# A first modulation computed on TensorE, between the first products, instead of on VectorE

## The chip, the cores and the metric

The kernel runs on one core of one Trainium2 chip. The metric is the device time of one execution in microseconds (us), as the median of several runs. One core has a matrix engine (TensorE, PE in the profile; its weight loads are listed apart as PEld), a vector engine (DVE), an activation engine (ACT), a general engine (POOL) and a sync engine (SP), which here only issues loads from the chip's memory. Each engine works off its own instructions in a fixed order and waits on semaphores for the others.

## The reference

Two small transformers run one after the other on a sequence of 512 positions with 1024 features, two layers each, in float32. Only the first one matters here:

```python
def first_block(x, c, positions, ada_w, ada_b, norm1_g, w_in, b_in, ...):
    cond = jax.nn.silu(c)
    for l in range(DEPTH):                       # 2 layers
        mod = (cond @ ada_w[l] + ada_b[l])[:, None, :]
        sh1, sc1, g1, sh2, sc2, g2 = jnp.split(mod, 6, axis=-1)
        h = rmsnorm(x, norm1_g[l]) * (1 + sc1) + sh1
        x = x + g1 * hybrid_mixer(h, cos, sin, w_in[l], b_in[l], ...)
        h = rmsnorm(x, norm2_g[l]) * (1 + sc2) + sh2
        x = x + g2 * swiglu(h, w_ffn_in[l], w_ffn_out[l])
```

`hybrid_mixer` projects h with `w_in` and runs three kinds of attention. One of them picks its keys by scores of index queries `qi` (four blocks of 128 features) against one index key `ki`, both rotated by position (`partial_rope`). The modulation `mod` has 6 x 1024 values, 48 groups of 128; the first normalization needs 16 of the groups, `sh1` and `sc1`.

## The kernel before, in words

Activations lie transposed, features on the partitions in 8 tiles (k = 0 to 7) of 128, positions along the free axis. A product in float32 precision is done as three: every operand is split into a rounded part ("hi") and the rest ("lo"), and hi x hi, lo x hi and hi x lo are added up in PSUM (`mm3`, L497). A *unit* is one block of 128 output features: 8 tiles x 3 = 24 matmuls of 128x512. Weights come as `w_raw` in loads of 512 KB; ACT rounds them (`w_hi`), DVE takes the difference (`w_lo`).

The order of each engine's instructions is written by hand: a list of `Op`s is worked off by `run_plan`, which lets weight preparation run ahead, and work that has to follow an evacuation at a distance is put off with `later(us, ...)` on a clock that the planner keeps. Buffers come from two arenas in SBUF, `ar` (57 slots of 512 rounded values) and `af` (45 slots of 256 values); `Slots.get` (L125) picks the free slot that was dropped first. Loads are issued on SP's queue in planned order, some on ACT's and POOL's.

The places that the change touches:
- `ada_ops` (L808): one group of `mod` is one load of 128 rows of the transposed `ada_w` (512 KB) and one DVE reduction over 128x1024 against `silu(c)`, which lies on all partitions (`spread_cond`). This is `CUSTOM_DVE_ANT_0` in the rows.
- `entry` (L1526), the start of layer 0. The input is loaded, transposed on PE and its row norms are made. Then for each tile k: two groups of `mod`, two small operations that make scale and shift (`ab`), one DVE multiplication of the tile (`norm_tile`, L741), the rounding on ACT and the lo part on POOL. `products` (L1544) holds the first five units together: 120 matmuls, three units for k = 0 and 1, then the other two, then all five tile by tile. These five units are `ki` and the four `qi`. Their first weights are prepared by ACT, DVE and POOL.
- `evac_turned` (L947): a `qi` unit that is done is copied out of PSUM by ACT and then rotated by `turn` (L936): four DVE multiplications of 32x512 by `sin_t` and two POOL operations with `cos_t`; `rest`, 6.5 us later on the planner's clock, splits it into hi and lo. In layer 1 the same units follow the end of layer 0.
- `spill` (L1136): the input tiles go to memory as `x_dram`, on POOL's queue.

The `Timed` helper records every operation, so all rows carry its line, L336 (L342 in the changed kernel); the rows are told apart by their tiles.

Of the kernel before, what the change touches and what calls it, by code (L numbers as in the profile page):

```python
# [98 lines left out]
ZO = 1  # L99
VG = 0  # L100
# [12 lines left out]
ROOM = 0  # L113


class Slots:


    def __init__(self, base, n, align=False):
        self.base, self.align = base, align  # L120
        self.free = [True] * n
        self.since = [0] * n
        self.now = 0

    def get(self, n=1):  # L125
# [3 lines left out]
        while i < len(self.free):  # L129
# [6 lines left out]
            for a in range(i, e - n + 1):  # L136
                if a % step == 0:
                    r = (a if n >= 8 else a < LOW and not self.align, self.broken(a, n) if self.align else 0,
                         max(self.since[a:a + n]))
                    if best is None or r < best[0]:  # L140
                        best = (r, a)
# [17 lines left out]
class Slot:  # L159
# [5 lines left out]
    def drop(self):  # L165
        for j in range(self.i, self.i + self.n):
            assert not self.pool.free[j]
            self.pool.free[j] = True
            self.pool.since[j] = self.pool.now = self.pool.now + 1
# [191 lines left out]
def tile_forward(ctx, tc, t, out):  # L361
# [13 lines left out]
    R, F = Slots(ar, NR, True), Slots(af, NF)  # L375

    def new(cols):
# [27 lines left out]
           (("m", 16), ("a0", 117), ("a1", 117), ("b0", 69), ("b1", 69))}  # L405
# [429 lines left out]
    def start_loads():  # L835
# [13 lines left out]
        columns("a0", 117, at=st["xs"][0].ap)  # L849
# [5 lines left out]
        spread_cond("cond", t["c"], q, False)  # L855
        st["load"](0, 2)
        st["load"](1, 3)
        st["hold"] = True
        rotary()

# [86 lines left out]
    def evac_turned(bias, dst, eng=None):  # L947
        def done(_, p):
            T = new(512)
            act(T.ap, p, AF.Identity, bias=bias)  # L950

            turn(T.ap, eng)
# [7 lines left out]
            later(6.5 if eng else 8.5, rest, dst)  # L960
# [185 lines left out]
    def block1_layer(l, ada, close):  # L1146
# [13 lines left out]
        def ki_done(_, p):  # L1160
            T, U = new(512), new(512)
            act(T.ap, p, AF.Identity, bias=vc[:, 77:78])
            later(1.5, lambda: ki_rest(T, U), ki)

        def ki_rest(T, U):
# [16 lines left out]
            later(7.0, rest, ki)  # L1182
# [343 lines left out]
    def entry(units):  # L1526

        vc = vec["a0"]
        def stats():
            act(scr, one_c, AF.Silu)  # L1530
            rows_stats(st["rows"], 0, junk, between)

        def between():
            act(st["cond"].ap, st["cond"].ap, AF.Silu)
            rows_turn(st.pop("rows"), st["x"], range(8))
        plan = [Op(0.0, start_loads), Op(0.0, stats), norm_spread(XW), Op(0.0, rotary_sin)]
        for u in units[:EP]:
# [5 lines left out]
        plan.append(Op(0.0, begin))  # L1543
        def products():  # L1544
# [3 lines left out]
            for k in range(2):  # L1548
                for u in units[:3]:
                    u.mms(k, k + 1, 0)  # L1550
            for u in units[3:]:
                u.mms(0, 2, 0)
            for k in range(2, 6):
                for u in units:
                    u.mms(k, k + 1, 0)
            for u in units:
                u.mms(6, KT, 0)
# [3 lines left out]
        def tile_op(k):  # L1561
            def run():
                nc.vector.scalar_tensor_tensor(ab[:, 0, k:k + 1], mod[:, 0, 8 + k:9 + k], 1.0, vc[:, k:k + 1],
                                               op0=OP.add, op1=OP.mult)
                nc.vector.tensor_copy(ab[:, 1, k:k + 1], mod[:, 0, k:k + 1])
                lo = norm_tile(XW, k, st["tmp"][k % 2].ap, st["tmp"][2 + k % 2].ap if k < HL else None)
                lo()
                if k == KT - 1:
                    st.pop("rx")
                    for s in st.pop("tmp"):  # L1570
                        s.drop()
            return Op(0.0, run)
        for k in range(KT):
            plan += ada(2 * k + 2, 16)
            plan.append(tile_op(k))
# [828 lines left out]
```

## Time and profile before

| | |
|---|---|
| median of 3 runs | 3311.58 us (3309.7 to 3319.43) |
| profiled execution | 3316.53 us, of which 3314.8 us from the first to the last instruction |
| PE busy | 3191.6 us (96%) |
| DVE busy | 2086.4 us (63%) |
| ACT busy | 1246.1 us (38%) |
| POOL busy | 526.8 us (16%) |
| mean granted TensorE clock | 0.978 of 2.4 GHz |

The page gives every engine's busy time, the span in 40 slices, the loads, the chain of work that ended last and the costliest groups. Its chain of waits is mostly PE: 56% of the span. PE is idle for 123 us of the span (3314.8 less 3191.6). A granted clock of 0.50 is 1.2 GHz, 1.00 is 2.4 GHz, and a stretch with a value between has some time at each.

### The profile page before, as it was taken

How to read it: one execution, taken by the hardware profiler on the slowest of the kernel's cores; microseconds unless marked ns; L12 is line 12 of the kernel's file. 1: busy time of each engine (PE TensorE's matmuls, PEld its weight loads, DVE VectorE, ACT ScalarE, POOL GpSimd, SP SyncE). 2: the span in 40 equal slices, each digit the busy share in tenths (PEclk: the TensorE clock that was granted, in tenths of full speed). 3: DMA queues.
4: the chain of work that ended last, by engine and by line, in shares of the span. 5: the costliest groups of instructions: out<-in, count | busy, mean ns of one | idle time of the engine just before them, and what ended most of it. 6: DMA issues, size and time to landing. Idle time of an engine off the chain costs nothing.

```text
span 3314.8 us, 42542 instructions
## 1 busy us (share of the span) xinstructions
PE 3191.6 (96%) x16663; PEld 2688.9 (81%) x16663; DVE 2086.4 (63%) x3632; ACT 1246.1 (38%) x2147; POOL 526.8 (16%) x431
## 2 busy tenths in 40 slices
PE   6899999999989999999999998899999999989999
PEld 4788788888878787798888887788888887778888
DVE  8777665566578864458885665566666655664443
ACT  4544324222245452242224454342222244543333
POOL 3233001000022410010002562100000046300001
PEclk8999999999999999999999999999999999999999
DMA  6211352465431112335553112133333221223222
GB/s 241 68 67 51 122 208 97 171 220 213 138 114 63 56 52 83 127 113 185 195 203 129 52 34 72 52 108 117 122 122 121 94 100 42 77 71 102 96 96 77
DMA packets 109068, 370.19 MB, mean 112 GB/s; under 512 B 12352, under 2 KB 13124, under 8 KB 108484
## 3 DMA queue, kind: packets, MB, share of 16 engines
q1 hardware_dynamic: 99778, 339.65, 29.7%
q0 software_dynamic: 5328, 20.97, 1.7%
q10 hardware_dynamic: 3762, 6.86, 0.7%
q8 instruction: 131, 2.15, 0.3%
q14 instruction: 69, 0.57, 0.1%
HBM read 354.85 MB, written 12.58 MB: 111 GB/s over the span
## 4 chain that ended last, share of the span: by engine, by line
PE 56%; DVE 5%; ACT 2%; issue 1%; POOL 0%; DMA 0%; ACTq 0%; DVEq 0%; POOLq 0%
PE ps L336 56%; DVE ar L336 2%; DVE af L336 2%; ACT af L336 1%; ACT ar L336 1%; DVE junk L336 1%; DVE w_lo L336 0%; ACT w_hi L336 0%; POOL af L336 0%; DMA w_raw<-in_win_dram 0%; DVE small L336 0%; DVE osum L336 0%; DMA af<-in_lam_dram 0%; ACT L336 0%; ACT osum L336 0%
## 5 line engine op out<-in xcount | busy, mean ns | idle before, releaser
L336 PE MATMUL ps<-ar,w_hi 128*128 128x512 f32 (+2 forms) x8248 | 2385.1, 371 | 48.7 <-DVE ar L336 23.3
L336 PEld LDWEIGHTS ps<-ar,w_hi 128*128 128x128 f32 (+1 forms) x8248 | 1499.9, 190 | 326.5 <-DVE ar L336 27.0
L336 PE MATMUL ps<-ar,w_lo 128*128 128x512 f32 (+2 forms) x4124 | 1512.3, 368 | 2.7 <-DVE w_lo L336 2.7
L336 PEld LDWEIGHTS ps<-ar,w_lo 128*128 128x128 f32 (+1 forms) x4124 | 782.4, 190 | 122.2 <-DVE w_lo L336 3.1
L336 DVE TENSOR_TENSOR w_lo<-w_raw,w_hi 128x1024 fp32r<-128x1024 f32 (+3 forms) x414 | 477.2, 1156 | 223.4 <-ACT w_hi L336 221.9
L336 ACT ACTIVATE w_hi<-w_raw 128x1024 fp32r<-128x1024 f32 (+3 forms) x452 | 440.1, 977 | 441.9 <-PE ps L336 391.8
L336 PE MATMUL ps<-ar 128*128 128x256 f32 (+6 forms) x3096 | 504.2, 331 | 28.2 <-ACT ar L336 13.8
L336 PEld LDWEIGHTS ps<-ar 128*128 128x128 f32 (+1 forms) x3096 | 423.0, 194 | 102.8 <-issue 19.0
L336 POOL TENSOR_TENSOR af<-af 128x512 f32<-128x512 f32 (+5 forms) x151 | 178.6, 1185 | 1646.3 <-ACT af L336 1623.2
L336 DVE SCALAR_TENSOR_TENSOR af<-ps,mod,af 128x512 f32<-128x512 f32 (+1 forms) x257 | 165.2, 646 | 263.9 <-PE ps L336 263.9
L336 ACT ACTIVATE ar<-af 128x512 fp32r<-128x512 f32 (+2 forms) x216 | 128.3, 599 | 439.4 <-DVE af L336 432.5
L336 ACT ACTIVATE af<-ps 128x512 f32<-128x512 f32 (+2 forms) x290 | 142.1, 516 | 376.1 <-PE ps L336 372.1
L336 DVE TENSOR_TENSOR ar<-af,ar 128x512 fp32r<-128x512 f32 (+2 forms) x202 | 144.5, 718 | 120.2 <-ACT ar L336 120.2
L336 DVE TENSOR_TENSOR ar<-ps,ar 128x512 fp32r<-128x512 f32 (+3 forms) x212 | 131.8, 648 | 84.8 <-ACT ar L336 84.1
L336 POOL TENSOR_TENSOR af<-af,sin_t 32x512 f32<-32x512 f32 x104 | 151.2, 1453 | 144.4 <-ACT af L336 61.8
L336 ACT ACTIVATE ar<-ps 128x512 fp32r<-128x512 f32 (+3 forms) x212 | 113.2, 568 | 98.6 <-PE ps L336 96.4
L336 DVE TENSOR_TENSOR af<-af 128x512 f32<-128x512 f32 (+2 forms) x130 | 80.4, 619 | 109.1 <-ACT af L336 104.4
L336 DVE CUSTOM_DVE_ANT_0 af<-af,vec_a 128x1024 f32<-128x1024 f32 x96 | 123.0, 1290 | 34.2 <-DMA af<-in_ada_w_dram 33.9
L336 ACT ACTIVATE af<-af 128x256 f32<-128x256 f32 (+2 forms) x134 | 70.7, 538 | 179.5 <-DVE af L336 162.9
L336 DVE CUSTOM_DVE_ANT_0 junk<-af,vec_b 128x1024 bf16<-128x1024 f32 x96 | 122.7, 1278 | 12.2 <-DMA af<-in_w_ada_dram 12.2
L336 DVE CUSTOM_DVE_ANT_0 af<-af,vec_b 128x1024 f32<-128x1024 f32 x96 | 123.3, 1285 | 3.4
L336 PE MATMUL ps<-ident,af 128*128 128x128 f32 (+2 forms) x733 | 104.6, 280 | 19.9 <-DMA af<-in_vec_a_dram 5.9
(128 smaller groups left out, 1702.5 us busy)
## 6 DMA issues: line engine op xcount, KB each, us to landing
w_raw<-in_win_dram SPq DMA_DIRECT2D x138, 512.0 KB, 3.3
af<-in_ada_w_dram SPq DMA_DIRECT2D x96, 512.0 KB, 4.4
af<-in_w_ada_dram SPq DMA_DIRECT2D x96, 512.0 KB, 4.4
w_raw<-in_wm_dram SPq DMA_DIRECT2D x96, 512.0 KB, 3.3
w_raw<-in_wfi_dram SPq DMA_DIRECT2D x88, 512.0 KB, 3.6
w_raw<-in_wfo_dram SPq DMA_DIRECT2D x48, 384.0 KB, 3.1
w_raw<-in_wm_dram SPq DMA_DIRECT2D x32, 320.0 KB, 3.3
x_dram<-af POOLq DMA_DIRECT2D x16, 512.0 KB, 4.2
```

The lines of the kernel that those rows point to most:

```text
L336: r = f(*a, **k)
```

## The change

The 16 groups of `sh1` and `sc1` of layer 0 are computed by matmuls. A new layout `ada_first` of the same weights has the contracted index on the partitions, so a group is eight matmuls with a 128x128 block of the weights as the stationary operand and one column of `silu(c)` (`cc`, part of the tile `small`) as the moving one: 128 matmuls of 128x1. All 16 results stand in one PSUM bank. They are written between the first products, two after each 128x512 matmul, and the products are placed tile by tile between the tile operations. The lo part of the tiles and of the first weights is made by DVE alone; POOL has none of it. `silu(c)` on all partitions, which the other groups still need, is loaded after the entry.

Besides, `evac_turned` puts off the `turn` of the four `qi` units by 0, 3, 6 and 9 us of the planner's clock, and `Slots` picks a slot by the time at which the planner expects it to be free. The second gives many tiles other slots all through the kernel.

```diff
-                    r = (a if n >= 8 else a < LOW and not self.align, self.broken(a, n) if self.align else 0,
+                    late = max(0.0, max(self.since[a:a + n]) - self.clocks.at["act"])
+                    r = (a if n >= 8 else a < LOW and not self.align, round(late, 1) if late > LATE else 0.0,
+                         self.broken(a, n) if self.align or n < 3 else a % 3 if n == 3 else 0, late,
                          max(self.since[a:a + n]))
                     if best is None or r < best[0]:
...
     def drop(self):
+        at = self.pool.clocks.ready((), (self.ap,))
         for j in range(self.i, self.i + self.n):
             assert not self.pool.free[j]
             self.pool.free[j] = True
-            self.pool.since[j] = self.pool.now = self.pool.now + 1
...
-        spread_cond("cond", t["c"], q, False)
-        st["load"](0, 2)
+        st["first"] = deque()
+        first_ada(2)
         st["load"](1, 3)
         st["hold"] = True
         rotary()
+    FIRST = [c for k in range(KT) for c in (8 + k, k)]
+    def first_ada(n):
+        while st.get("fetched", 0) < n:
+            i = st["fetched"] = st.get("fetched", 0) + 1
+            s = new(1024)
+            nc.sync.dma_start(s.ap, t["ada_first"][FIRST[i - 1]])
+            st["first"].append(s)
     def rows_stats(rows, sc, junk, between=None):
...
-    def evac_turned(bias, dst, eng=None):
+    def evac_turned(bias, dst, eng=None, wait=0.0):
         def done(_, p):
             T = new(512)
             act(T.ap, p, AF.Identity, bias=bias)
-
-            turn(T.ap, eng)
             dst.pair = Pair(R)
             h, l = dst.pair.hi, dst.pair.lo
...
-            later(6.5 if eng else 8.5, rest, dst)
+            def middle():
+                turn(T.ap, eng)
+                later(RE if eng else 8.5, rest, dst)
+            later(wait, middle, dst) if wait else middle()
         return done
...
-                        evac(vc[:, 64 + i:65 + i], box, *((nc.vector,) if 9 <= i < 13 else ())))
+                        evac(vc[:, 64 + i:65 + i], box, *((nc.vector, RW + RS * (i - 9)) if 9 <= i < 13 else ())))
...
     def entry(units):
         vc = vec["a0"]
+        cc = small[:, 224:232]
+        b1 = small[:, 232:240]
         def stats():
             act(scr, one_c, AF.Silu)
-            rows_stats(st["rows"], 0, junk, between)
-
-        def between():
-            act(st["cond"].ap, st["cond"].ap, AF.Silu)
-            rows_turn(st.pop("rows"), st["x"], range(8))
-        plan = [Op(0.0, start_loads), Op(0.0, stats), norm_spread(XW), Op(0.0, rotary_sin)]
-        for u in units[:EP]:
-            u.w.rest = (nc.vector, nc.gpsimd)
+            act(cc, vc[:, 117:125], AF.Silu)
+            nc.vector.tensor_scalar(b1, vc[:, 24:32], 1.0, None, op0=OP.add)
+            rows = st.pop("rows")
+            rows_stats(rows, 0, junk)
+            rows_turn(rows, st["x"], range(8))
         def begin():
-            st["tmp"] = [new(S) for _ in range(4)]
+            st["tmp"] = [new(S) for _ in range(2)]
+            first_ada(6)
             new_h()
...
             st["entry"] = False
+            st["mods"] = bank("st")
+            open_banks.add(turns["last"])
+            st["mods_at"] = turns["last"]
             for u, tg in zip(units, ["acc", "acc", "pv", "st", "st"]):
                 u.open(0, tg)
...
+        def modulate(k):
+            p = st["mods"]
+            for i in (2 * k, 2 * k + 1):
+                w = st["first"].popleft()
+                for j in range(KT):
+                    nc.tensor.matmul(p[:, i:i + 1], w.ap[:, 128 * j:128 * j + 128], cc[:, j:j + 1],
+                                     start=j == 0, stop=j == KT - 1)
+                    yield
+                w.drop()
+            first_ada(min(16, 2 * k + 8))
+        def products(k, us, other=()):
+            other = iter(other)
+            h, l = hm(k)
+            for u in us:
+                for j, (w, x) in enumerate(((u.w.h, h), (u.w.l, h), (u.w.h, l))):
+                    nc.tensor.matmul(u.ps[0], w[k], x, start=k + j == 0, stop=k == KT - 1 and j == 2)
+                    next(other, None)
+                    next(other, None)
+            for _ in other:
+                pass
+        def tile_op(k):
+            nc.vector.scalar_tensor_tensor(ab[:, 0, k:k + 1], st["mods"][:, 2 * k:2 * k + 1], b1[:, k:k + 1], vc[:, k:k + 1],
+                                           op0=OP.add, op1=OP.mult)
+            nc.vector.tensor_add(ab[:, 1, k:k + 1], st["mods"][:, 2 * k + 1:2 * k + 2], vc[:, 16 + k:17 + k])
+            norm_tile(XW, k, st["tmp"][k % 2].ap)()
+            if k == KT - 1:
+                st.pop("rx")
+                for s in st.pop("tmp"):
+                    s.drop()
+        hm = hmove(lambda: h_box["h"])
+        def last():
+            open_banks.discard(st.pop("mods_at"))
+            st.pop("mods")
             for u in units:
-                u.mms(6, KT, 0)
+                for k in (KT - 2, KT - 1):
+                    products(k, [u])
+                open_banks.discard(u.at[0])
                 u.w.drop()
                 u.done(0, u.ps[0])
...
+        def step(f, *a):
+            return Op(0.0, lambda: f(*a))
+        some, rest = units[:3], units[3:]
+        plan = [Op(0.0, start_loads), Op(0.0, stats), Op(0.0, begin), step(lambda: deque(modulate(0)))]
+        plan += [norm_spread(XW), step(tile_op, 0), Op(0.0, lambda: None, pre=[u.w for u in some])]
+        plan += [Op(0.0, lambda: st["load"](1, 5)), step(lambda: deque(modulate(1))), step(tile_op, 1)]
+        for k in range(KT - 2):
+            if k == 1:
+                plan += [Op(0.0, lambda: None, pre=[u.w for u in rest])]
+            if k == 2:
+                plan += [step(products, 0, rest), step(products, 1, rest)]
+            if k == 3:
+                plan += [Op(0.0, lambda: st.pop("hold")), Op(0.0, rotary_sin)]
+            plan.append(step(lambda k=k: products(k, some if k < 2 else units, modulate(k + 2))))
+            plan.append(step(tile_op, k + 2))
         plan += [Op(0.0, spill), Op(0.0, rotary_end)]
-        plan += [Op(26.0, products, [u.w for u in units]), Op(0.0, more_consts)]
+        plan += [Op(26.0, last, [u.w for u in units]), Op(0.0, more_consts), Op(0.0, lambda: spread_cond("cond", t["c"]))]
         return plan
...
-        order = [c for k in range(KT) for c in (8 + k, k)] + list(range(16, 48)) if l == 0 else range(48)
+        order = range(16 if l == 0 else 0, 48)
...
-    todo, done = deque(adas), [0]
+    todo, done = deque(adas), [16]
...
+    o["ada_first"] = lay(a["ada_w"][:1, :, :2048], 8)[0]
...
+        if l == 0:
+            o["vec_a0"] = np.concatenate([o["vec_a0"], v(a["c"])])
```

PE's first rows, before: the transposed column vectors and input tiles, the spread of the norms, and the 120 products in one piece, then the first of the next unit (`w_hi`).

```order
L336 MATMUL ps<-ident,af 128x117
L336 MATMUL ps<-ident,af 128x128 x32
L336 MATMUL ps<-ident,stat 128x128 x4
L336 MATMUL ps<-ar 128x512 x120
L336 MATMUL ps<-ar,w_hi 128x512
```

And now, where `small` is the tile that holds `silu(c)` and `af` the modulation's weights:

```order
L342 MATMUL ps<-ident,af 128x125
L342 MATMUL ps<-ident,af 128x128 x32
L342 MATMUL ps<-small,af 128x1 x16
L342 MATMUL ps<-ident,stat 128x128 x4
L342 MATMUL ps<-small,af 128x1 x16
L342 MATMUL ps<-ar 128x512
L342 MATMUL ps<-small,af 128x1 x2
```

Groups of 16 narrow matmuls (one tile's scale and shift) stand ahead of the norms, behind them, and then in pairs between the products of k = 0 to 5: nine products with 16 narrow ones for k = 0 and again for k = 1, then 12 products of the other two units in a row, then 15 with 16 for each of k = 2 to 5, and 30 products alone for k = 6 and 7.

DVE's rows after the entry in layer 0, before: weights' lo parts, all four turns but one in a row (`sin_t`, four operations each), two small constants, the index weights `wf`, the last turn, and the lo part of a value unit that frees its PSUM bank (`ar<-ps`).

```order
L336 TENSOR_TENSOR w_lo<-w_raw,w_hi 128x1024 x2
L336 TENSOR_TENSOR af<-af,sin_t 32x512 x16
L336 CAST cmask_b<-af 128x128
L336 CAST ident_b<-ident 128x128
L336 TENSOR_TENSOR w_lo<-w_raw,w_hi 128x1024
L336 COPY wf<-ps 128x64
L336 TENSOR_SCALAR wsc<-wf 128x32
L336 TENSOR_TENSOR af<-af,sin_t 32x512 x4
L336 SCALAR_TENSOR_TENSOR ar<-ps,vec_a_95,ar 128x512
```

And now:

```order
L342 TENSOR_TENSOR w_lo<-w_raw,w_hi 128x1024 x2
L342 TENSOR_TENSOR af<-af,sin_t 32x512 x4
L342 CAST cmask_b<-af 128x128
L342 CAST ident_b<-ident 128x128
L342 TENSOR_TENSOR w_lo<-w_raw,w_hi 128x1024
L342 COPY wf<-ps 128x64
L342 TENSOR_SCALAR wsc<-wf 128x32
L342 TENSOR_TENSOR af<-af,sin_t 32x512 x8
L342 SCALAR_TENSOR_TENSOR ar<-ps,vec_a_95,ar 128x512
L342 TENSOR_TENSOR w_lo<-w_raw,w_hi 128x1024
L342 TENSOR_TENSOR ar<-af,ar 128x512
L342 TENSOR_TENSOR af<-af,sin_t 32x512 x4
```

Twelve `sin_t` operations stand ahead of the first `ar<-ps` where 20 stood.

DVE at the start of layer 1, before, from the first turns to the lo part that frees a bank:

```order
L336 TENSOR_TENSOR af<-af,sin_t 32x512 x8
L336 TENSOR_TENSOR w_lo<-w_raw,w_hi 128x1024
L336 TENSOR_TENSOR af<-af,sin_t 32x512 x4
L336 COPY wf<-ps 128x64
L336 TENSOR_SCALAR wsc<-wf 128x32
L336 TENSOR_TENSOR af<-af,sin_t 32x512 x4
L336 TENSOR_TENSOR w_lo<-w_raw,w_hi 128x1024
L336 TENSOR_TENSOR af<-af,sin_t 32x512 x4
L336 TENSOR_TENSOR ar<-af,ar 128x512 x2
L336 TENSOR_TENSOR w_lo<-w_raw,w_hi 128x1024
L336 TENSOR_TENSOR ar<-af,ar 128x512
L336 COPY af<-af 64x512
```

And now, the same stretch:

```order
L342 TENSOR_TENSOR af<-af,sin_t 32x512 x4
L342 TENSOR_TENSOR w_lo<-w_raw,w_hi 128x1024
L342 COPY wf<-ps 128x64
L342 TENSOR_SCALAR wsc<-wf 128x32
L342 TENSOR_TENSOR af<-af,sin_t 32x512 x8
L342 TENSOR_TENSOR w_lo<-w_raw,w_hi 128x1024
L342 TENSOR_TENSOR ar<-af,ar 128x512
L342 TENSOR_TENSOR w_lo<-w_raw,w_hi 128x1024
L342 TENSOR_TENSOR af<-af,sin_t 32x512 x4
L342 COPY af<-af 64x512
L342 TENSOR_TENSOR ar<-af,ar 128x512 x2
L342 SCALAR_TENSOR_TENSOR ar<-ps,vec_a_95,ar 128x512
```

The second `w_lo` stands behind 12 turn operations instead of 16, and the `ar<-ps` behind 16 instead of 20.

## Rows read from the trace of the kernel before

**Rows 1.** Page, the span in 40 slices: PE busy, and granted clock.
```profile
PE   6899999999989999999999998899999999989999
PEclk8999999999999999999999999999999999999999
```

**Rows 2.** Windows: busy us of PE, PEld, DVE, ACT, POOL; clock, DMA share, GB/s.
```profile
0.00:20.00 20.00, 7.67 (x37) 6.79 (x37) 10.26 (x27) 13.72 (x21) 0.20 (x4) 0.89 0.87 325
20.00:40.00 20.00, 9.89 (x18) 5.10 (x18) 18.03 (x25) 7.12 (x12) 10.48 (x6) 0.50 0.59 215
...
sum 120.00, PE 83.35 PEld 63.61 DVE 95.69 ACT 54.57 POOL 41.09; mean PE 13.89 PEld 10.60 DVE 15.95 ACT 9.10 POOL 6.85
```

**Rows 3.** Timeline of DVE in the entry: start, us, count, [idle before <- releaser].
```profile
22.28 4.73 DVE L336 TENSOR_TENSOR ar<-w_raw,ar 128x512 fp32r<-128x512 f32 x3 [1.92 <-ACT ar L336]
...
41.94 3.15 DVE L336 TENSOR_TENSOR ar<-w_raw,ar 128x512 fp32r<-128x512 f32 x4 [1.92 <-ACT ar L336]
...
48.27 1.28 DVE L336 CUSTOM_DVE_ANT_0 af<-af,vec_a 128x1024 f32<-128x1024 f32 x1
...
50.68 1.25 DVE L336 SCALAR_TENSOR_TENSOR ab<-mod,vec_a 128x1 f32<-128x1 f32 x1
...
51.96 0.75 DVE L336 SCALAR_TENSOR_TENSOR af<-af,ab,ps 128x512 f32<-128x512 f32 x1
...
55.03 1.24 DVE L336 SCALAR_TENSOR_TENSOR ab<-mod,vec_a 128x1 f32<-128x1 f32 x1
```

**Rows 4.** Timeline of PE in the entry and right after it.
```profile
22.30 0.79 PE L336 MATMUL ps<-ar 128*128 128x512 f32 x1 [4.09 <-ACT ar L336]
...
43.34 18.49 PE L336 MATMUL ps<-ar 128*128 128x512 f32 x74 [0.58 <-DVE ar L336]
...
64.34 5.94 PE L336 MATMUL ps<-ar 128*128 128x512 f32 x25 [1.23 <-POOL ar L336]
70.12 0.39 PE L336 MATMUL ps<-ar,w_hi 128*128 128x512 f32 x1
```

**Rows 5.** Timeline of PE at eight narrow matmuls.
```profile
550.66 0.95 PE L336 MATMUL ps<-mean_c,af 128*128 128x1 f32 x8
551.48 0.36 PE L336 MATMUL ps<-ar,w_hi 128*128 128x256 f32 x1
```

**Rows 6.** Windows at two packs of 16 narrow matmuls, columns as in Rows 2.
```profile
1814.70:1818.00 3.30, 2.71 (x25) 2.66 (x24) 2.12 (x2) 2.25 (x5) 1.04 (x1) 0.98 0.05 20
1818.00:1821.40 3.40, 3.40 (x17) 3.40 (x17) 1.53 (x12) 0.30 (x1) 0.00 (x0) 0.50 0.83 281
```

**Rows 7.** Timeline after the entry: turns on DVE, and PE's wait.
```profile
66.96 17.17 DVE L336 TENSOR_TENSOR af<-af,sin_t 32x512 f32<-32x512 f32 x16 [0.46 <-ACT af L336]
...
91.53 0.79 PE L336 MATMUL ps<-ar,w_hi 128*128 128x512 f32 x1 [9.76 <-DVE ar L336]
...
92.12 0.63 PE L336 MATMUL ps<-ar,w_lo 128*128 128x512 f32 x1
...
92.55 1.05 PE L336 MATMUL ps<-ar,w_hi 128*128 128x512 f32 x2
```

**Rows 8.** Window of PE's first matmuls behind that wait.
```profile
91.50:98.00 6.50, 6.47 (x16) 5.12 (x17) 6.27 (x7) 0.74 (x2) 2.75 (x2) 0.54 0.26 83
```

**Rows 9.** Timeline of DVE at the start of layer 1.
```profile
964.75 4.74 DVE L336 TENSOR_TENSOR af<-af,sin_t 32x512 f32<-32x512 f32 x4
...
976.52 0.75 DVE L336 SCALAR_TENSOR_TENSOR ar<-ps,vec_a,ar 128x512 fp32r<-128x512 f32 x1
```

**Rows 10.** Timeline of PE at the start of layer 1.
```profile
964.77 0.80 PE L336 MATMUL ps<-ar,w_lo 128*128 128x512 f32 x1 [2.70 <-DVE w_lo L336]
...
977.32 0.80 PE L336 MATMUL ps<-ar,w_hi 128*128 128x512 f32 x1 [5.55 <-DVE ar L336]
```

**Rows 11.** Windows at the start of layer 1.
```profile
962.00:968.00 6.00, 3.30 (x9) 2.56 (x9) 5.90 (x6) 0.61 (x2) 3.86 (x2) 0.72 0.28 98
976.00:985.00 9.00, 7.68 (x25) 6.21 (x26) 4.89 (x6) 3.45 (x5) 0.00 (x0) 0.69 0.40 147
```

More of the change, by code (lines that the diff above doesn't have):

```diff
@@ L99 @@
 ZO = 1
+LATE = 1.0
+RW, RS, RE = 0.0, 3.0, 6.5
+KW, KE = 1.5, 7.0
 VG = 0
@@ L112, with __init__ @@
 L0, L1 = 5.0, 8.0
-ROOM = 0
+ROOM, FROOM = 0, 0
 class Slots:
-    def __init__(self, base, n, align=False):
+    def __init__(self, base, n, clocks, align=False):
         self.base, self.align = base, align
@@ L122, in __init__ @@
         self.since = [0] * n
-        self.now = 0
+        self.clocks = clocks
     def get(self, n=1):
@@ L168, in drop @@
             self.pool.free[j] = True
-            self.pool.since[j] = self.pool.now = self.pool.now + 1
+            self.pool.since[j] = at
 class Pair:
@@ L374, in tile_forward @@
     af = arena.tile([128, NF, 256], FT, name="af")
-    R, F = Slots(ar, NR, True), Slots(af, NF)
+    R, F = Slots(ar, NR, clocks, True), Slots(af, NF, clocks)
     def new(cols):
@@ L404, in tile_forward @@
     vec = {n: const.tile([128, k], FT, name="vec_" + n) for n, k in
-           (("m", 16), ("a0", 117), ("a1", 117), ("b0", 69), ("b1", 69))}
+           (("m", 16), ("a0", 125), ("a1", 117), ("b0", 69), ("b1", 69))}
     mod = const.tile([128, 2, 48], FT, name="mod")
@@ L848, in start_loads @@
                                        ap=[[0, 128], [1, S]]))
-        columns("a0", 117, at=st["xs"][0].ap)
+        columns("a0", 125, at=st["xs"][0].ap)
         nc.vector.memset(quarter, math.pi / 2.0)
@@ L1162, in ki_done @@
             act(T.ap, p, AF.Identity, bias=vc[:, 77:78])
-            later(1.5, lambda: ki_rest(T, U), ki)
+            later(KW, lambda: ki_rest(T, U), ki)
         def ki_rest(T, U):
@@ L1181, in rest @@
                 U.drop()
-            later(7.0, rest, ki)
+            later(KE, rest, ki)
         u_ki = Unit(W(win[13], keep=True, rest=None), hm, XS, ki_done)
@@ L1540, in begin @@
         def begin():
-            st["tmp"] = [new(S) for _ in range(4)]
+            st["tmp"] = [new(S) for _ in range(2)]
+            first_ada(6)
             new_h()
-        plan.append(Op(0.0, begin))
-        def products():
             st["entry"] = False
+            st["mods"] = bank("st")
+            open_banks.add(turns["last"])
+            st["mods_at"] = turns["last"]
             for u, tg in zip(units, ["acc", "acc", "pv", "st", "st"]):
                 u.open(0, tg)
[L1548 to L1555, printed above, removed]
+        def modulate(k):
[8 more added lines that the diff above has]
+            first_ada(min(16, 2 * k + 8))
@@ L1556, in products @@
+        hm = hmove(lambda: h_box["h"])
+        def last():
+            open_banks.discard(st.pop("mods_at"))
+            st.pop("mods")
             for u in units:
-                u.mms(6, KT, 0)
+                for k in (KT - 2, KT - 1):
+                    products(k, [u])
+                open_banks.discard(u.at[0])
                 u.w.drop()
                 u.done(0, u.ps[0])
[L1561 to L1572, printed above, removed]
@@ L1573, in entry @@
-        for k in range(KT):
-            plan += ada(2 * k + 2, 16)
-            plan.append(tile_op(k))
-            if k == 0:
-                plan.append(Op(0.0, lambda: None, pre=[u.w for u in units[:3]]))
-            if k == HW:
-                plan.append(Op(0.0, lambda: st["load"](1, 5)))
-            if k == HU:
-                plan += [Op(0.0, lambda: None, pre=[u.w for u in units[3:]]), Op(0.0, lambda: st.pop("hold"))]
+        def step(f, *a):
+            return Op(0.0, lambda: f(*a))
@@ L2257, in mixed @@
                         late = wait(o)
-                        if late < 0.15 or wait(f) > late or sum(R.free) < ROOM or sum(F.free) < ROOM:
+                        if late < 0.15 or wait(f) > late or sum(R.free) < ROOM or sum(F.free) < FROOM:
                             break
```

## The prediction

> **What bounds the kernel now.** I began with the page's slices: PE is busy nearly throughout, and only the first two slices stay well below [rows 1]. The windows then say how much is in the start: PE works 83.35 of the first 120 us, so 36.65 of its 123 idle us lie in under 4% of the span, and the clock is 0.50 all through 20 to 40 us [rows 2]. In a stretch like that the question is what PE waits for, so next came DVE's timeline there. One tile of the entry costs DVE two reductions of 1.28 us, a scale of 1.25, a copy and a multiplication of 0.75, and scale follows scale after 55.03 - 50.68 = 4.35 us [rows 3]. PE gets its products only as tiles come: the first at 22.30, a run without a break from 43.34, the next units' weights at 70.12 [rows 4]. Behind the entry DVE makes 16 turn operations in one go and PE waits 9.76 us [rows 7]; the same pattern returns in layer 1 with waits of 2.70 and 5.55 us [rows 10]. These places are what the change touches; over the rest of the span PE hardly stops.
>
> **Prices.** Eight matmuls of 128x1, each with its own 128x128 weights, took 551.48 - 550.66 = 0.82 us, 0.103 each, at full clock [rows 5]. In a window at 0.50 seventeen matmuls, half of them of that kind, filled 3.40 us: 0.20 each [rows 6]. A 128x512 matmul starts 0.43 after the one before at half clock (92.12 to 92.55) [rows 7], and 25 of them took 5.94 us at full clock, 0.238 with the last one's tail [rows 4]; half of 0.43 is 0.215, and I take 0.227 between.
>
> **The entry.** Removed are 16 reductions of 1.28 us, 20 us of DVE, and POOL's share of the lo parts. Added are 128 narrow matmuls: 13 us of PE at full clock, 26 at half. Three of DVE's operations per tile remain and the lo part joins them, at most 1.25 + 0.14 + 0.75 + 0.75 = 2.9 us where the period was 4.35 [rows 3], so DVE no longer sets the pace once the weights are split. PE does, and its clock decides:
> - The first 16 narrow matmuls stand ahead of the spread of the norms, at half clock 3.2 us; the first tile no longer waits for two reductions (2.56 us). I put the first product at 22.7, 0.4 later than before.
> - The second product stands behind a pair of narrow matmuls that write the bank DVE reads for the second tile's scale, and in DVE's queue that scale stands behind six lo parts of weights. Shared with POOL such a part took 4.73 / 3 = 1.58, alone 3.15 / 4 = 0.79 [rows 3]; POOL has none now, so six are 4.7 us and PE goes on at about 27.8. Nothing covers this wait.
> - k = 0 and k = 1: 9 x 0.43 + 16 x 0.20 = 7.1 us each at half clock, to 42.0.
> - Then 12 wide matmuls alone. Before, the clock came up in the unbroken run from 43.34: 74 products in 18.49 us, 0.25 each [rows 4]. I expect the same here: 12 x 0.43 = 5.2, with the rise near their end, to 46.8.
> - k = 2 to 5 at full clock: 15 x 0.227 + 16 x 0.103 = 5.05 each, to 67.0; the last 30 take 6.8, to 73.8.
> Before, this point came at 70.12: the entry gets 3.7 us longer. DVE's 20 us were not all on the path, PE had 36 us to spare, but the spare time lay where the clock was at 0.50.
>
> Loads: the third tile's two groups are the thirteenth load of 512 KB on SP; at 325 GB/s [rows 2] 6.8 MB take 21 us. The spill of the input tiles to memory (four writes of 512 KB) no longer stands behind POOL's lo parts and goes out among them; with it the sum is 8.9 MB and 27.4 us, just in time for 27.8. I take nothing for it; if the next four loads shared the time as well, 11.0 MB and 33.8 us, it would be 6 us late, the upper bound.
>
> **Behind the entry, layer 0.** PE's third unit needs the lo part that frees its bank, and 12 turn operations stand ahead of it on DVE instead of 20. One costs 17.17 / 16 = 1.07 us beside POOL [rows 7]: 8 x 1.07 = 8.6 us earlier, against a wait of 9.76. What is late next is the fourth unit: its lo parts now stand behind a bundle of four (4.3 us). I count half of that as given back, 8.6 - 2.1 = 6.5 gained. The bounds are 4.3 (all given back) and 11.8: 16 matmuls behind the wait ran at 0.54 [rows 8], and if the wait gets short enough for the clock to stay up, 16 x 0.20 = 3.2 come on top. The late load of silu(c) and its two ACT operations stand behind the entry while DVE sets the pace there, so nothing for them.
>
> **Layer 1.** The second lo part stands behind 12 turn operations instead of 16. At 4.74 / 4 = 1.19 us [rows 9] that is 4.7 us earlier, and the wait of 2.70 goes [rows 10]. The unit before then ends some 5 us sooner; on DVE come one lo part, one `w_lo`, the last bundle (4.7) and four short ones ahead of the `ar<-ps` that ended at 977.27 [rows 9]. Walking this queue I get 969.5 for it and 967.5 for PE: a wait of 2 us is left of 5.55, so 3.5 gained. In the windows there, 9 matmuls took 3.30 us and 25 took 7.68 [rows 11]; at 0.227 they would take 2.0 and 5.7, another 3.3 for the clock. Sum 9.5 us. Bounds: 2.7 (only the first wait) and 13.
>
> **The slots.** Other slots change waits all over the kernel. Outside the places above PE idles about 123.2 - 36.65 - 8.25 = 78 us, spread over many small waits that no rule here takes away or adds. I count 0, and 5% of it, 4 us, either way as an estimate.
>
> **Sum.** 3.7 - 6.5 - 9.5 + 0 = -12.3 us. On the profiled execution: 3316.53 - 12.3 = 3304.2. That execution was 4.95 us above the median of 3311.58, so the same saving from the median gives 3299.3; I predict 3299. What counts as no change is 0.3%, 9.9 us, so the forecast lies just past the edge.
>
> **Rivals.**
> - *The clock stays down in the entry; slower.* Place: the products of k = 2 to 5. If the 12 wide matmuls don't bring it to 1.00, or the narrow ones between push it back, each of four tiles costs 15 x 0.43 + 16 x 0.20 = 9.65 instead of 5.05, and about ten of the last 30 run at 0.43: 18.4 + 2.0 = 20.4 more, 3299.3 + 20.4 = 3319.7. It gets slower than before from the point where three of the four tiles run at half. For it: with a pack of narrow matmuls, PE busy 2.71 of 3.30 us, the clock went from 0.98 to 0.50 and stayed there while more of them were mixed in [rows 6]. Against it: in those packs nothing wide stood between, here one wide matmul takes as long as the two narrow ones, and the run ahead of them is wide alone. Chance 0.13.
> - *The clock rises at once; faster.* If it comes up within k = 0, some 3 us into it, the rest of k = 0 takes 2.3, k = 1 takes 9 x 0.227 + 16 x 0.103 = 3.7, the 12 take 2.7, and all from there as above: the end comes near 67, about 7 earlier, 3292. For it: PE has no idle time from 27.8 on. Against it: rows 6 again, and the half clock through 20 to 40 us in spite of short bursts [rows 2]. The Trainium skill speaks for this one: "TensorE: Matmul & The Clock Gate", Part 1 (the HAM clock gate), says that the gate is set by how busy PE has been recently, and a stream of narrow matmuls is busy. By that rule the time would be 3292; the trace does not agree, since PE was busy 82% of the window in which its clock was lost. Chance 0.15.
> - *The queue only moves.* DVE still has 20 turn operations to make before the index scores, and made 16 in 17.17 us without a break [rows 7]. If every bundle that leaves one place delays a `w_lo` or an `ar<-ps` at the next, only the first wait of layer 1 goes: 3311.6 + 3.7 - 2.7 = 3312.6. For it: in both layers the bundles still stand ahead of the lo parts in the order. Against it: from layer 1's third unit on PE has wide units of 24 matmuls, 5.4 us each, and a bundle is 4.3 to 4.7. Chance 0.18.
> - *The slots decide.* A wait of some 10 us appears or goes where no row points: 3289 or 3309. Chance 0.10, half each.
>
> **How the numbers follow.** The forecast's own case has 0.44, with its own range of 3291 to 3307: the bounds of the two turn terms, not all at once, and 4 us for the slots. In it the time is below 3301.7 (0.3% under the median) two times in three. Faster: 0.29 + 0.14 from the early clock + 0.06 from slots + 0.01 = 0.50. Slower: 0.07 from the late clock, 0.02 from the queue, 0.02 from slots = 0.11. The rest, 0.39, is within 0.3%. The range that leaves out about one in ten on each side goes from 3285, the early clock with the full gain behind the entry, to 3318, just short of the late clock.
>
> **What would show it.** In the profile after: the first product near 22.7 and the second near 27.8; the clock 0.50 until about 46 and 1.00 from there; the first `w_hi` product of the later units near 74; PE's wait behind the first two units at 2 to 4 us instead of 9.76; the first wait of layer 1 gone, the second about 2. The prediction is wrong if the granted clock is 1.00 before 40 or still 0.50 at 52, if a load releases the narrow matmuls, or if the waits on `ar<-ps` are as long as before.

## The result, and the profile after

The changed kernel takes 3347.1 us (median of 4 runs, 3345.59 to 3350.22) where the kernel before, timed beside it, takes 3315.51: a ratio of 1.0097 with a 95% interval of 1.0076 to 1.0119. 32 us slower, where 3299 was predicted and 3318 was the upper end of the range.

The page's slices look better than before, and that is the trap in them: PE is busy for 8 tenths of each of the first two slices, where [rows 1] had 6 and 8, but the granted clock is a tenth lower in both.

```profile
PE   8899999999999999999999998899999999989999
PEclk7899999999999999999999999999999999989999
```

The windows (columns as in [rows 2]) show PE without a pause from 20 to 100 us, and 106.71 us busy of the first 120 where 83.35 were needed before. The time is not lost in waits; PE has more to do, and much of it at half clock.

```profile
20.00:40.00 20.00, 20.00 (x88) 19.08 (x87) 7.15 (x14) 4.56 (x8) 0.00 (x0) 0.50 0.82 328
40.00:60.00 20.00, 20.00 (x85) 17.82 (x84) 5.92 (x12) 3.52 (x6) 0.00 (x0) 0.60 0.23 80
60.00:80.00 20.00, 20.00 (x122) 17.85 (x122) 5.26 (x12) 5.22 (x7) 0.00 (x0) 0.91 0.37 132
80.00:100.00 20.00, 20.00 (x90) 16.69 (x90) 7.97 (x14) 6.06 (x8) 2.57 (x2) 0.83 0.25 78
sum 120.00, PE 106.71 PEld 94.33 DVE 50.20 ACT 36.06 POOL 13.68; mean PE 17.79 PEld 15.72 DVE 8.37 ACT 6.01 POOL 2.28
```

PE's timeline in the entry, beside [rows 4], tells what it has to do. The reader should compare the counts with the order of the change: there a tile's pack is x16 and a pair is x2, here they are x32 and x4.

```profile
15.82 6.96 PE L342 MATMUL ps<-small,af 128*128 128x1 f32 x32 [2.86 <-ACT af L342]
22.64 1.09 PE L342 MATMUL ps<-ident,stat 128*128 128x128 f32 x4
23.53 6.83 PE L342 MATMUL ps<-small,af 128*128 128x1 f32 x32
30.22 0.77 PE L342 MATMUL ps<-ar 128*128 128x512 f32 x1
30.79 0.95 PE L342 MATMUL ps<-small,af 128*128 128x1 f32 x4
31.60 0.77 PE L342 MATMUL ps<-ar 128*128 128x512 f32 x1
...
51.23 5.64 PE L342 MATMUL ps<-ar 128*128 128x512 f32 x14
56.71 0.50 PE L342 MATMUL ps<-small,af 128*128 128x1 f32 x4
...
85.72 10.72 PE L342 MATMUL ps<-ar 128*128 128x512 f32 x37
96.28 0.39 PE L342 MATMUL ps<-ar,w_hi 128*128 128x512 f32 x1
```

The list of groups (busy us, mean ns) counts them all: 128 matmuls of the program stand in the trace as 256, each with a weight load of its own (PEld).

```profile
L342 PE MATMUL ps<-small,af 128*128 128x1 f32 x256 | 44.5, 285 | 2.9 <-ACT af L342 2.9
L342 PEld LDWEIGHTS ps<-small,af 128*128 128x128 f32 x256 | 51.9, 268 | 6.6 <-ACT af L342 3.1 <-DVE ab L342 0.2
```

The first product with `w_hi` starts at 96.28 instead of 70.12 [rows 4]: 26.2 of the 32 us are gone before the entry's end. Behind it, PE's waits on the way to layer 0's index scores and at the start of layer 1, beside [rows 7] and [rows 10]. The second line is the four transposes of the third unit's result, a value unit; they stand just ahead of the index scores and waited for nothing before.

```profile
111.71 0.80 PE L342 MATMUL ps<-ar,w_hi 128*128 128x512 f32 x1 [3.78 <-DVE ar L342]
...
128.22 1.11 PE L342 MATMUL ps<-ident,af 128*128 128x128 f32 x4 [6.09 <-ACT af L342]
...
1002.66 0.80 PE L342 MATMUL ps<-ar,w_hi 128*128 128x512 f32 x1 [4.62 <-DVE ar L342]
```

The wait of 9.76 has become 3.78, but a new one of 6.09 stands 17 us behind it. In layer 1 the wait of 2.70 is gone and that of 5.55 is 4.62.

To see where each kernel gains or loses, I matched the products with `w_hi` by their number (8248 in every trace) and took the start of each against the kernel before, in us. Each row is one profiled execution; behind layer 1 the steps vary by some 3 us between kernels that are alike there, so the last column says less than the timed ratios.

| kernel | entry's end | third unit | behind the third unit's transposes | before layer 1's waits | behind them | last |
|---|---|---|---|---|---|---|
| changed kernel | +26.2 | +20.2 | +27.3 | +30.8 | +26.0 | +31.7 |
| slots alone | -0.1 | +2.0 | +1.7 | +2.1 | +1.7 | +9.7 |
| turns alone | +0.1 | -1.8 | +3.5 | +3.8 | -1.5 | +4.3 |
| slots and turns | 0.0 | -1.9 | +3.9 | +6.6 | +1.2 | +3.4 |
| changed, turns not put off | +33.0 | +35.0 | +34.0 | +36.3 | +36.6 | +41.4 |
| changed, half the narrow ones | +0.9 | -5.0 | +2.2 | +4.5 | -0.8 | +6.1 |
| changed, an eighth of them | -11.4 | -15.9 | -8.8 | -7.5 | -13.4 | -8.8 |
| turns of layer 1 alone | +0.1 | +0.1 | -1.3 | -2.6 | -9.1 | -7.5 |
| and turns 3, 4 of layer 0 | -0.1 | -6.8 | -1.7 | -4.0 | -9.2 | -6.4 |
| and turn 4 later still | +0.1 | -6.7 | -6.3 | -4.9 | -11.3 | -13.2 |

### The profile page after: what moved, and what is told of

The parts are those of the page before. It is cut to its first block, busy times and chain, and to the rows that moved or that the text cites. A ratio compares the mean times of both kernels' runs of the same rounds, so it can differ in the third digit from the quotient of the medians.

```text
span 3346.6 us, 42991 instructions
## 1 busy us (share of the span) xinstructions
PE 3235.9 (97%) x16919; PEld 2738.2 (82%) x16919; DVE 2046.9 (61%) x3612; ACT 1245.2 (37%) x2141; POOL 503.0 (15%) x420
## 4 chain that ended last, share of the span: by engine, by line
PE 83%; DVE 6%; ACT 3%; POOL 2%; issue 1%; DMA 0%; ACTq 0%; DVEq 0%; POOLq 0%
PE ps L342 83%; DVE af L342 3%; DVE ar L342 2%; POOL af L342 2%; ACT af L342 1%; ACT ar L342 1%; DVE w_lo L342 1%; ACT w_hi L342 1%; DVE junk L342 1%; ACT L342 0%; DVE osum L342 0%; DVE small L342 0%; DMA w_raw<-in_win_dram 0%; DMA af<-in_lam_dram 0%; ACTq L342 0%
## 5 line engine op out<-in xcount | busy, mean ns | idle before, releaser
L342 PE MATMUL ps<-ar 128*128 128x256 f32 (+6 forms) x3096 | 514.6, 332 | 14.5 <-DVE ar L342 7.1
L342 PE MATMUL ps<-ident,af 128*128 128x128 f32 (+2 forms) x733 | 105.7, 283 | 27.3 <-ACT af L342 11.9
L342 DVE CUSTOM_DVE_ANT_0 af<-af,vec_a 128x1024 f32<-128x1024 f32 x80 | 102.1, 1280 | 37.3 <-DMA af<-in_ada_w_dram 37.1
```

The costliest lines, as they stand in the source:

```text
L342: r = f(*a, **k)
```

## The experiments

My theory after the result: a 128x1 product in float32 runs as two passes, each with its own weight load, so the entry has 256 and not 128 narrow matmuls to place, and that is what it loses. Rivals: the new choice of slots or the turns lose it over the kernel; or the half clock of the entry costs it whatever the count; or the entry's new order does, with its lo parts made by DVE alone.

**The parts apart.** Slots alone, on the kernel before:

```diff
-                    r = (a if n >= 8 else a < LOW and not self.align, self.broken(a, n) if self.align else 0,
+                    late = max(0.0, max(self.since[a:a + n]) - self.clocks.at["act"])
+                    r = (a if n >= 8 else a < LOW and not self.align, round(late, 1) if late > LATE else 0.0,
...
-            self.pool.since[j] = self.pool.now = self.pool.now + 1
+            self.pool.since[j] = at
```

> The kernel before with only the new choice of slots. Theory 1 (the loss is made in the entry, by narrow matmuls that run as two passes each): slots alone are worth nothing beyond 4 us, so 3311 to 3320 where the kernel before has 3315. Rival (the slots spread waits over the whole kernel): the 5 to 6 us that were lost outside the entry and the turns come back here, 3320 to 3326.

Measured: a ratio of 1.0027 (1.0017 to 1.0036), 3327.78 against 3318.38. By the interval the slots alone cost 6 to 12 us. The time itself lies above both expectations, but these were set beside 3315; counted from the kernel before, the rival (5 to 11 us more) held. 3.7 us of it appear at one place of layer 1. There ACT empties six index scores; before, it did so in one go (2.39 us for the six), and now it stops in between for DVE's work on a buffer of `af`. A value unit's transposes wait behind it on PE, and the clock falls behind that wait (ACT's and PE's timeline, then windows):

```profile
1012.74 0.60 ACT L341 ACTIVATE af<-ps 128x512 f32<-128x512 f32 x1 [2.01 <-DVE af L341]
1013.39 0.99 PE L341 MATMUL ps<-ident,af 128*128 128x128 f32 x4 [1.99 <-ACT af L341]
```

```profile
1010.00:1013.40 3.40, 0.65 (x7) 0.43 (x6) 1.92 (x2) 1.32 (x3) 2.10 (x1) 1.00 0.11 24
1013.40:1018.50 5.10, 5.10 (x18) 4.21 (x19) 2.84 (x5) 2.18 (x6) 0.00 (x0) 0.67 0.24 87
```

The same pair of waits, 2.01 on ACT and 1.99 on PE, stands at the index scores of layer 0 in the changed kernel (PE at 154.24) and in three of the runs below that have the new slots: slots and turns (131.69), half (129.68) and an eighth (119.22). No kernel with the old slots has it.

The turns alone, on the kernel before (`evac_turned` as in the change):

```diff
-                        evac(vc[:, 64 + i:65 + i], box, *((nc.vector,) if 9 <= i < 13 else ())))
+                        evac(vc[:, 64 + i:65 + i], box, *((nc.vector, RW + RS * (i - 9)) if 9 <= i < 13 else ())))
```

> The kernel before with only the four turns put off by 0, 3, 6 and 9 us. By the prediction's two terms: 6.5 us gained in layer 0 and 9.5 in layer 1, 3299. Rival (the queue only moves, as the new waits of 6.1 us on PE and of 13.8 us on ACT behind the third unit of layer 0 suggest): gains of 6 and 5 us, 7 given back, 3311 to 3315.

Measured: 0.9993 (0.9983 to 1.0002), no difference. The rival was right. The table says how: behind the third unit's transposes in layer 0 it is 3.5 us late, in layer 1 it gains 5.3. The trace shows why layer 0 does not gain (DVE, then PE):

```profile
67.10 2.77 DVE L337 TENSOR_TENSOR af<-af,sin_t 32x512 f32<-32x512 f32 x4 [0.49 <-ACT af L337]
77.86 0.23 DVE L337 CAST cmask_b<-af 128x128 bf16<-128x128 f32 x1 [7.99 <-DMA af<-in_cst_dram]
...
89.78 0.79 PE L337 MATMUL ps<-ar,w_hi 128*128 128x512 f32 x1 [7.87 <-DVE ar L337]
104.36 1.12 PE L337 MATMUL ps<-ident,af 128*128 128x128 f32 x4 [5.11 <-ACT af L337]
```

With only one turn in front of it, DVE stands 8 us before a constant that ACT's queue loads; before, three more turns filled that time. Put-off work went into the time when DVE was needed. In the changed kernel, where the entry ends later, the wait for this constant is 2.98.

Both together, with the entry of before:

> The whole change but the entry, which is the one of before. Theory 1: the entry alone makes the loss of 26 us, so this one is 26 below the changed kernel, about 3321, with the 5 us above before left to turns and slots. By the prediction's terms without the entry: 3299. Rival (the three parts hang together): above 3327.

Measured: 1.0007 (0.9998 to 1.0017), 3320.87 against 3318.38, as theory 1 had it. That it fits to the microsecond is luck, since the kernel before took 3315.51 beside the changed kernel and 3318.38 here. All but the entry is worth nothing together within the interval, and the entry has the loss, a ratio of 1.0097 with it and 1.0007 without.

The changed kernel with the turns not put off (`RS = 0.0`):

> The changed kernel with the turns not put off. Theory 1: the 26 us of the entry stay, and the gains and losses of the turns go: 3341 to 3350. Rival (the turns put off are what loses behind the entry, 7 us in the wait of ACT): 3335 to 3340.

Measured: 1.0106 (1.0079 to 1.0133), 3357.16 with a single run at 3340.66: above both expectations. In the profiled execution the entry itself is 7 us longer (+33.0), and 8.4 us more are lost behind it, where the changed kernel loses 5.5; so no loss by the turns shows. The 7 us can't come from the turns, because PE's instructions up to the entry's end are the same in both kernels. The windows show that the clock makes them: in the mixed stretch it swings between its two levels, and here (first fence) more of it lies at the lower one than in the changed kernel (second fence). Why the swings differ stays open.

```profile
60.00:70.00 10.00, 10.00 (x48) 8.82 (x47) 1.75 (x4) 3.77 (x5) 0.00 (x0) 0.67 0.62 236
70.00:80.00 10.00, 10.00 (x48) 8.82 (x47) 1.75 (x4) 0.72 (x1) 0.00 (x0) 0.67 0.00 1
```

```profile
60.00:70.00 10.00, 10.00 (x67) 9.04 (x67) 2.71 (x7) 3.77 (x5) 0.00 (x0) 1.00 0.74 262
70.00:80.00 10.00, 10.00 (x57) 8.81 (x56) 2.55 (x6) 1.45 (x2) 0.00 (x0) 0.83 0.01 2
```

**The count.** Half of the narrow matmuls; the planner is told of all, so that the order of everything else stays:

```diff
-                    nc.tensor.matmul(p[:, i:i + 1], w.ap[:, 128 * j:128 * j + 128], cc[:, j:j + 1],
-                                     start=j == 0, stop=j == KT - 1)
+                    if j % 2:
+                        clocks.matmul(p[:, i:i + 1], w.ap[:, 128 * j:128 * j + 128], cc[:, j:j + 1])
+                    else:
+                        nc.tensor.matmul(p[:, i:i + 1], w.ap[:, 128 * j:128 * j + 128], cc[:, j:j + 1],
+                                         start=j == 0, stop=j == KT - 2)
```

> The changed kernel with every second narrow matmul left out (half of the modulation's sum is missing), the planner's account of them kept, so that all else stands in the same order. Theory 1 (each narrow f32 product is two passes, PE is the limit of the entry): 128 passes fewer, 64 of them before the twelve wide products at 0.21 us and 64 behind at 0.09 to 0.1, 13.6 + 6.1 = 20 us less, and the clock no longer falls at 77 and 84: the entry's products end at 72 to 77 instead of 96, 3322 to 3328 in all, which is what was predicted for the full count. Rival (the half clock of the entry is what costs, whatever the count): the clock stays at 0.50 until 50 and the end comes at 85 or later, 3336 or more.

Measured: 3323.09, a ratio of 1.0022 (1.0010 to 1.0034). The trace has 128 narrow matmuls, and the first `w_hi` product starts at 71.03 where 72 to 77 was expected; the clock comes up near 42 and stays:

```profile
22.30:31.00 8.70, 7.22 (x26) 6.04 (x26) 3.69 (x8) 1.48 (x3) 0.00 (x0) 0.50 1.03 421
31.00:38.20 7.20, 7.20 (x26) 6.33 (x27) 4.16 (x8) 2.80 (x5) 0.00 (x0) 0.50 1.02 406
38.20:43.50 5.30, 5.30 (x17) 4.21 (x17) 1.75 (x4) 0.72 (x1) 0.00 (x0) 0.62 0.33 113
43.50:71.00 27.50, 27.50 (x154) 23.70 (x153) 12.78 (x24) 10.49 (x14) 0.00 (x0) 1.00 0.36 127
```

This is nearly the entry that the prediction described, in its 128 matmuls and in its clock. It takes 0.9 us longer than before; 3.7 was the forecast. The difference is DVE's six lo parts, which were to hold the second product until 27.8. They run in part ahead of the first product, and PE waits only 1.48 us behind it (PE's timeline, from that wait on):

```profile
24.58 0.58 PE L342 MATMUL ps<-small,af 128*128 128x1 f32 x2 [1.48 <-DVE ab L342]
25.02 0.77 PE L342 MATMUL ps<-ar 128*128 128x512 f32 x1
```

The kernel as a whole is still slower than the one before, by 3 to 11 us, although 12.3 us less were forecast with such an entry. So the entry is not all that the prediction had wrong.

One of eight left (`if j:` in the place of `if j % 2:`, and one matmul that both starts and stops):

> As the half, with one of eight narrow matmuls left (seven eighths of the modulation's sum are missing). Theory 1: 224 passes fewer, 112 x 0.21 + 112 x 0.095 = 34 us at most; the entry's products can't end before DVE's lo parts and the 120 products allow, so 60 to 66, and 3310 to 3316 in all. Rival (loads set the pace: the last of the sixteen groups lands near 45): the end stays above 70.

Measured: 3310.01, a ratio of 0.9982 (0.9972 to 0.9993), in the expected range. The first `w_hi` product starts earlier than the expectation's 60:

```profile
58.67 0.39 PE L342 MATMUL ps<-ar,w_hi 128*128 128x512 f32 x1
```

Loads held PE for 1.6 us and DVE for 3.7 in this entry, none of it behind 35 us. With 256, 128 and 32 matmuls in the trace the entry ends at 96.3, 71.0 and 58.7: the count decides, with the clock that goes with it. Both runs keep the entry's new order and DVE's lo parts, so these two don't cost the 26 us.

**Versions that keep what gained.** Since layer 1 gained and layer 0 lost, the turns were put off in layer 1 only, with slots and entry of before:

```diff
-                        evac(vc[:, 64 + i:65 + i], box, *((nc.vector,) if 9 <= i < 13 else ())))
+                        evac(vc[:, 64 + i:65 + i], box, *((nc.vector, l * (RW + RS * (i - 9))) if 9 <= i < 13 else ())))
```

> The kernel before with the turns put off in layer 1 only. From the run with the turns alone: layer 0 lost 5.3 us by the index scores and layer 1 gained 5.3, so without the part in layer 0 about 5 us less than the kernel before, a ratio of 0.998 to 0.999. Rival (layer 1's gain is given back behind it, as 4 us were lost behind 2250 us there): no difference, a ratio of 0.9995 or more.

Measured: 0.9974 (0.9964 to 0.9984), 3309.82 against 3318.9: faster than the kernel before, and by more than the expectation's 0.998. 6.5 us come from layer 1's waits; the expectation had 5. The table's 2.6 us ahead of layer 1 were not followed.

Then in layer 0 the third and fourth turn as well (`RS * (i - 9) * (l or i > 10)`):

> As the run before, and in layer 0 only the third and fourth turn put off, so that DVE has eight turn operations ahead of the constant it waits for and not four. If DVE's wait for that constant (8.0 us idle behind the first turn) is what took layer 0's gain: the third unit of PE starts near 86 instead of 91.5, the ACT no longer stands before a late turn when the fourth unit ends, and 8 to 10 us less than before in all, a ratio of 0.997. Rival (the bundles only move): the wait at the index scores stays, 3 us or less beside the run with layer 1 alone.

Measured: 0.9975 (0.9966 to 0.9985), so nothing on top: the rival. The first half of my expectation held, the third unit of PE starts at 84.74, but the gain is gone by that unit's transposes. There ACT, which works in order, stands before an operation that waits for a copy behind the fourth turn on DVE, and the evacuation that PE waits for stands behind it on ACT (DVE, ACT, PE in turn):

```profile
92.30 4.28 DVE L337 TENSOR_TENSOR af<-af,sin_t 32x512 f32<-32x512 f32 x4
96.61 0.42 DVE L337 COPY af<-af 64x512 f32<-64x512 f32 x1
```

```profile
97.13 0.63 ACT L337 ACTIVATE ar<-af 128x512 fp32r<-128x512 f32 x1 [8.91 <-DVE af L337]
97.66 1.04 ACT L337 ACTIVATE w_hi<-w_raw 128x1024 fp32r<-128x1024 f32 x1
98.61 0.67 ACT L337 ACTIVATE af<-ps,vec_a 128x512 f32<-128x512 f32 x1
```

```profile
84.74 0.50 PE L337 MATMUL ps<-ar,w_hi 128*128 128x512 f32 x1 [3.04 <-DVE ar L337]
...
99.33 0.94 PE L337 MATMUL ps<-ident,af 128*128 128x128 f32 x4 [4.67 <-ACT af L337]
```

So the fourth turn was put behind that copy:

```diff
+                        evac(vc[:, 64 + i:65 + i], box, *((nc.vector, (RW + RS * (i - 9) if l else (0.0, 0.0, 6.0, 14.0)[i - 9])) if 9 <= i < 13 else ())))
```

> As the run before (third and fourth turn of layer 0 put off, all of layer 1), with the fourth turn of layer 0 put off by 14 instead of 9, so that on DVE it stands behind the copy of 64x512 that ACT waits for. If that wait of ACT (8.9 us) is what gives layer 0's gain back through PE's wait of 4.67 us at the next transposes: that wait goes, layer 0 keeps 5 to 6 of its 7 us, and the whole is 4 to 6 us below the run before, a ratio of 0.996 or less. Rival (DVE's queue as a whole is late, whatever its order): a wait of 3 us or more comes up at another unit of layer 0, and the ratio stays at 0.9975.

The mechanism is as expected: the copy starts at 92.40, and PE's wait of 4.67 is down to 0.83.

```profile
84.85 0.50 PE L337 MATMUL ps<-ar,w_hi 128*128 128x512 f32 x1 [3.00 <-DVE ar L337]
...
95.59 0.66 PE L337 MATMUL ps<-ident,af 128*128 128x128 f32 x4 [0.83 <-ACT af L337]
```

By the time it is not settled: 3307.26 against 3318.57, a ratio of 0.9970 (0.9954 to 0.9986), whose interval overlaps the two before; the profiled executions differ by 6.7 us (3308.3 and 3301.6 of span). It beats the kernel before; whether it beats the version with layer 1 alone stays open.

## Why the prediction was wrong

Two steps failed: the entry's sum, and the gain that I counted for the turns. The table adds up what is missing: 12.3 us less were forecast, and the profiled executions have 31.7 more, which is 44.0 apart. The entry has 22.5 of it (26.2 for 3.7). Layer 0 behind the entry has 11.1 (4.6 lost where 6.5 were to be gained), layer 1 has 4.7 (4.8 gained for 9.5), and 5.7 lie behind layer 1. The first alone puts the time outside the range, and so does the rest alone, as the run with half of the narrow matmuls shows.

**The larger step is the price of a narrow matmul in the sum of the entry.** I divided 0.82 us by the eight that [rows 5] count and multiplied by the 128 of the order. The trace's eight are passes, as are the packs of 16 in [rows 6], and the program's matmul is two of them. The evidence stood in the trace of before (groups by line): its rows have 180 + 80 = 260 narrow matmuls, the program has 130, all of them sums with the columns `mean_c` and `mean_v`, and I never set one number beside the other. Per pass the price was near: 32 took 6.96 us at half clock, 0.22 each, where I counted 0.20.

```profile
L336 PE MATMUL ps<-mean_c,af 128*128 128x1 f32 x180 | 23.8, 255 | 7.9 <-ACT af L336 5.6 <-POOL af L336 1.6 <-ACT stat L336 0.6
L336 PE MATMUL ps<-mean_v,af 128*128 128x1 f32 x80 | 10.7, 237 | 1.8 <-ACT af L336 1.1 <-DVE ar L336 0.4
```

The two packs ahead of the products end at 30.22 now, so the first product starts there and not at 22.7, and the second follows without a wait. With the count doubled the prediction's own formulas give, from 30.2 on: 2 x (9 x 0.43 + 32 x 0.20) = 20.5, 5.2 for the twelve, 4 x (15 x 0.227 + 32 x 0.103) = 26.8 and 6.8: the end at 89.5 instead of 73.8. Measured: 96.3. Of the remaining 6.8 us, 5.3 lie where the clock was lost once more (below) and the rest in small differences of each term.

**The clock, rival one, was half right.** The twelve wide products did bring it to 1.00 near their end, as forecast, but this end came at 56 instead of 47; still 0.50 at 52 was one of the prediction's own signs of being wrong. And with 32 narrow passes in a tile and not 16 the clock was lost again. The windows are those of the wide products, of the tiles k = 2, 3 and 4, of k = 5 without its last seven products, and of these seven with the last 30. They show 0.57, then 1.00 twice, and then 0.84, 0.76 and 0.79. By the prices at full clock the last three would take 6.7, 5.1 and 8.4 us; they took 8.3, 6.6 and 10.6, which is 1.6 + 1.5 + 2.2 = 5.3 more.

```profile
51.20:56.70 5.50, 5.50 (x15) 4.37 (x16) 1.75 (x4) 0.72 (x1) 0.00 (x0) 0.57 0.28 95
56.70:63.80 7.10, 7.10 (x50) 6.43 (x48) 1.02 (x4) 0.77 (x2) 0.00 (x0) 1.00 0.36 110
63.80:70.80 7.00, 7.00 (x48) 6.37 (x47) 1.74 (x4) 3.72 (x5) 0.00 (x0) 1.00 0.70 266
70.80:79.10 8.30, 8.30 (x49) 7.26 (x48) 2.51 (x5) 0.72 (x2) 0.00 (x0) 0.84 0.01 2
79.10:85.70 6.60, 6.60 (x40) 6.20 (x39) 0.00 (x0) 0.00 (x0) 0.00 (x0) 0.76 0.00 0
85.70:96.30 10.60, 10.60 (x39) 8.55 (x40) 7.61 (x12) 5.37 (x7) 0.27 (x1) 0.79 0.29 99
```

The rival that the clock rises at once was wrong: PE was busy 20.00 of 20 us from 20 to 40 at 0.50. The rule of the Trainium skill that spoke for it ("TensorE: Matmul & The Clock Gate", Part 1, the gate is set by how busy PE has been) does not agree with that row if busy is read as busy time.

**DVE's part.** That DVE no longer sets the pace was right: from 15.82 to 96.28 PE did not wait for DVE once. The six lo parts took 3.70 us (4.7 predicted), but the wait that I put behind the first product was not there, because the second pack covers it; in the run with half of the matmuls 1.48 us of it were left. Loads did not release a narrow matmul in the changed kernel.

**Behind the entry, layer 0: the second step that failed.** The first half was right: the third unit's wait fell to 3.78 (2 to 4 predicted) and 6.0 us were gained there (6.5 predicted). The 2.1 us that I let go for the fourth unit were too few, and the place was wrong: 7.1 us were lost at the third unit's transposes, through ACT's order. ACT stands 13.83 us before an operation that DVE's last turn and copy release, and the evacuation that PE needs stands behind it:

```profile
124.12 1.15 ACT L342 ACTIVATE ar<-af 128x512 fp32r<-128x512 f32 x2 [13.83 <-DVE af L342]
127.47 0.69 ACT L342 ACTIVATE af<-ps,vec_a 128x512 f32<-128x512 f32 x1 [1.26 <-DVE ar L342]
```

I had costed ACT's work behind the entry at nothing because DVE sets the pace there, and did not ask who waits behind ACT while ACT waits for DVE. That is the rival in which the queue only moves, in layer 0. The run with the fourth turn behind the copy shows it: there 6.3 us are still gained behind these transposes. Most of another 3.5 us, lost from there to layer 1, lies where the slots make ACT wait at the index scores.

**Layer 1.** The first wait went, as predicted. For the second I walked DVE's queue to 969.5 and PE to 967.5; shifted by the 30.8 us that the changed kernel is late there, they are at 971.8 and 967.2. ACT's share in that queue (0.76 and 1.51 us of waits on it) was left out. The wait that stayed is 4.62, and the clock fell behind it: the two windows of 7 us from 998 on have 0.74 and 0.77. 4.8 us gained in place of 9.5, inside its bounds.

**The slots** were no zero with 4 us either way: alone they cost 0.17 to 0.36%. In company with the turns this cost does not show (1.0007 against 0.9993, the intervals overlap). The wait of ACT at the index scores that comes with the new slots is one part of it; the rest of the cost, and why it does not add to that of the turns, stays open.

## What to carry to other kernels

Before a price per instruction is multiplied by a count, set the trace's count of some such instruction beside the program's: here 260 against 130 would have shown that each of these narrow float32 products is paid twice. An engine with idle time is a place for work only at the clock that it has there, and the 10 us in which PE was idle from 20 to 40 us here were at half clock [rows 2]. And when work is put off on one in-order queue, follow the next queue too: ask which operation on ACT waits for it, and what PE needs that stands behind that operation.

## What the runs showed of the hardware

- A matmul of 128x1 with plain float32 operands stood in the trace as two matmuls with two weight loads (256 of each for 128), 0.21 to 0.22 us each at half clock (6.96 us for 32). The float32 transposes by `ident` stood there once each (the four of `stat`, for one).
- Packs of such matmuls, and then four of them between two wide products, kept PE busy 20.00 of 20 us and left the granted clock at 0.50; two between two wide products left it there as well (31.00 to 38.20 in the run with half of them). In both kernels it rose in the run of wide products that followed. Once it was up, two passes between two wide products held it at 1.00 for 27.5 us; with four it was lost twice within 30 us.
